# The long convolutions of a hybrid layer, emitted in two lanes of blocks that take turns

## The chip, the core and the metric

The kernel runs on one core of a Trainium2 chip. Five engines have queues of their own and execute them strictly in order: PE (matrix multiplication, writes to PSUM), DVE (vector), ACT (scalar functions), POOL (here it mostly issues DMAs) and SP (issues DMAs only). They wait for each other through semaphores. PSUM has eight banks of 128 partitions x 512 fp32 values. The metric is the device time of one execution in microseconds; less is better.

## The reference

One layer of a diffusion backbone, in fp32, on 1024 latent tokens and 256 context tokens of width 1024. One input projection makes q, k, v for 8 attention heads and three signals x1, x2, v of 512 channels for a Hyena group. The two groups of heads are independent until their outputs are concatenated:

```python
proj = h @ w_in
a = attend(q, k, v)                       # neighbourhood attention + context keys
z   = x1 * long_conv(v, k_f[:, 0])        # the Hyena group, after a width-3 convolution
hyo = x2 * long_conv(z, k_f[:, 1])
merged = concat([rmsnorm(a), rmsnorm(hyo)])
x = x + g1 * (merged @ w_out)             # then a gated FFN and the final norm
```

`long_conv` is a convolution as long as the sequence, by way of a Fourier transform: transform, multiply with the filter's spectrum, transform back. Channels don't mix in it, so it splits into blocks of 128 channels.

## The kernel before, in words

The stages, in the order in which they are written: modulated norm of the tokens; input projection, with the filters' spectra beside it; long convolutions; attention; output projection; FFN. The functions don't run as written: each engine's queue is put in order by a scheduler that works through a model of the machine and takes, of the instructions that it holds ready, the one with the highest priority, which is the order of writing. `tc.high_priority(offset=CHP)` with CHP = 2000 moves what is inside it 2000 instructions forward in that order. So the long convolutions run partly beside the projections before them and partly beside the attention after them. Once the queues are set, they don't change: an instruction that waits holds up all that stands behind it on its engine.

**One block of the long convolution** is a call of `chain(j)`: j = 0 to 3 are the four blocks of 128 channels of the latent tokens, j = 4 is all channels of the context tokens (shorter, since it needs no radix-4 steps). A block does two convolutions after each other (o = 0, then o = 1, which takes the result of the first). Each of these ten *half chains* has four phases:

- forward: 8 matmul rows on PE into the PSUM tag `cA` (`pscA`, line 802), four banks' worth, each emptied by ACT (L805, L810, L814, L815) and DVE (L816) before the next can use the bank
- spectrum: radix-4 butterflies on DVE (L822 to L827), then the product with the filter's spectrum K, which comes from DRAM in two halves through one buffer per block parity (L836; L840 to L843 on DVE)
- inverse butterflies and twiddles (L847 to L852, L857 to L859)
- inverse: 8 matmul rows (line 871) into two banks' worth of `cA`, emptied through ACT and DVE with the gate x1 or x2 (L876 to L884); for o = 1 the result goes to DRAM as `hyd` (L889, L892).

The SBUF buffers (s8, s4, t, K) carry the block's parity j % 2 in their names, so two blocks in succession have buffers of their own.

**PSUM.** While the projections run, five banks belong to them (`psp` three, `pstB` two) and three to `cA`. Attention takes seven (`psav` one, `psS` four, `psX` two), so `cA` shrinks to one. The shrinking is written in the loop over the blocks: ahead of j = 2.

**Attention** (`attend`, four calls for two heads each): scores on PE (L1038), bias and maximum on DVE (L1059, L1066), exponentials on ACT (L1072, L1073), transposes on PE (L1082) whose results ACT and DVE copy (L991, L989), products with v on PE (L999). POOL issues the loads of the bias tables (L951), of q and of k. After the four calls `token_scales` (L1187 to L1196) makes the norms of the attention's output.

**Output projection** (`psd`, L116 to L118): 480 matmuls. Its weights `w_out` come into the SBUF space that the long convolutions held (`wo_split`, L1158 on ACT, L1159 on DVE), so their loads (L1166) wait for the last block's store.

Of the kernel before, what the change touches and what calls it, by code (L numbers as in the profile page):

```python
# [77 lines left out]
def build(tc, I, O, dbg=None, upto=99):  # L78
    nc = tc.nc
    V, A, G, T, Q = nc.vector, nc.scalar, nc.gpsimd, nc.tensor, nc.sync  # L80
    dbg = dbg or {}
    top = ExitStack()
    with top:
        _build(nc, tc, top, V, A, G, T, Q, I, O, dbg, upto)


def _build(nc, tc, top, V, A, G, T, Q, I, O, dbg, upto):
# [20 lines left out]
    def bk(tag):  # L108
        pl, n, bufs = banks[tag]
        return pl.tile([P, 512 * n], F32, tag=tag, name="ps" + tag, bufs=bufs)  # L110
# [22 lines left out]
    def tw_chain(h, r):  # L133
        b = (h * 3 + r - 1) * 3
        return tw[:, b:b + 1], tw[:, b + 1:b + 2], tw[:, b + 2:b + 3]
# [364 lines left out]
    with ies:  # L500
# [3 lines left out]
        for gi, (s, col, tl) in enumerate(groups):  # L504
            xs = []
            for i in tl:
                src, row, _ = tiles[i]
# [22 lines left out]
            n = P * len(tl)  # L530
# [238 lines left out]

    def chain(j):  # L770

        lat = j < 4
        b_ = j % 2

        def s8():
            return cp.tile([P, 2048], F32, tag=f"s8{b_}", name="s8", bufs=2)

        def s4(dt=F32):
            return cp.tile([P, 1024], dt, tag=f"s4{b_}", name="s4", bufs=S4B)

        f4 = "p (h i q c) -> p h i q c"
        v2 = "p (i x) -> p i x"
        src = lxd[j] if lat else cxd
        f1 = "p i x -> p (i x)"

        def load(which):
            t = s4()
            Q.dma_start(out=t, in_=src[which].rearrange(f1))
            return t

        u = load(0)
        for o in range(2):
            uv = u.rearrange(v2, i=2)
            Gt = s8()
            Gv = Gt.rearrange(f4, h=2, i=2, q=4)
            for h in range(2):
                hs = slice(h * P, (h + 1) * P)
                for rp in range(2):
                    pa = bk("cA")
                    xs = slice(rp * 256, (rp + 1) * 256)  # L800
                    for i in range(2):
                        T.matmul(pa[:, i * 256:(i + 1) * 256], dftf[:, i, hs], uv[:, i, xs], start=True, stop=True)
                    pv = pa.rearrange("p (i r c) -> p i r c", i=2, r=2)
                    if not lat:
                        A.copy(Gv[:, h, :, 2 * rp:2 * rp + 2], pv)  # L805
                        continue
                    for ri in range(2):
                        r = 2 * rp + ri
                        if r == 0:
                            A.copy(Gv[:, h, :, 0], pv[:, :, 0])  # L810
                            continue
                        c, s, ns = tw_chain(h, r)
                        t = cp.tile([P, 2, P], F32, tag=f"t{b_}", name="t", bufs=TB)
                        A.activation(t[:, 0], pv[:, 1, ri], AF.Copy, scale=ns)  # L814
                        A.activation(t[:, 1], pv[:, 0, ri], AF.Copy, scale=s)  # L815
                        V.scalar_tensor_tensor(Gv[:, h, :, r], pv[:, :, ri], c, t, op0=ALU.mult, op1=ALU.add)  # L816
            if lat:
                ac = s4().rearrange(f4, h=2, i=2, q=2)
                X = s8()
                Xv = X.rearrange(f4, h=2, i=2, q=4)  # L820
                Xf = X.rearrange("p (h x c) -> p h x c", h=2, x=8)
                V.tensor_add(ac, Gv[:, :, :, 0:2], Gv[:, :, :, 2:4])  # L822
                V.tensor_sub(Gv[:, :, :, 2:4], Gv[:, :, :, 0:2], Gv[:, :, :, 2:4])
                V.tensor_sub(Xf[:, :, 2:8:5], Gv[:, :, :, 2], Gv[:, :, ::-1, 3])
                V.tensor_add(Xf[:, :, 3:7:3], Gv[:, :, :, 2], Gv[:, :, ::-1, 3])
                V.tensor_add(Xv[:, :, :, 0], ac[:, :, :, 0], ac[:, :, :, 1])
                V.tensor_sub(Xv[:, :, :, 1], ac[:, :, :, 0], ac[:, :, :, 1])  # L827
                Y = Gt
            else:
                X = Gt  # L830
                Y = s8()
            Xs = X.rearrange("p (h i x) -> p h i x", h=2, i=2)
            Ys = Y.rearrange("p (h i x) -> p h i x", h=2, i=2)
            for h in range(2):
                Kt = cp.tile([P, 2, 512], F32, tag=f"K{b_}", name="K", bufs=1)
                Q.dma_start(out=Kt.rearrange(f1), in_=(Kd[o, j] if lat else Kc[o])[:, h * 1024:(h + 1) * 1024])  # L836
                kr = Kt[:, 0:1].to_broadcast([P, 2, 512])
                ki = Kt[:, 1:2].to_broadcast([P, 2, 512])
                B = s4().rearrange(v2, i=2)
                V.tensor_mul(B, Xs[:, h, ::-1], ki)  # L840
                V.tensor_mul(Ys[:, h], Xs[:, h], kr)
                V.tensor_sub(Ys[:, h, 0], Ys[:, h, 0], B[:, 0])
                V.tensor_add(Ys[:, h, 1], Ys[:, h, 1], B[:, 1])  # L843
            if lat:
                ac = s4().rearrange(f4, h=2, i=2, q=2)
                Gf = Gt.rearrange("p (h x c) -> p h x c", h=2, x=8)
                V.tensor_add(ac, Gv[:, :, :, 0:4:2], Gv[:, :, :, 1:4:2])  # L847
                V.tensor_sub(Xv[:, :, :, 0:2], Gv[:, :, :, 0:4:2], Gv[:, :, :, 1:4:2])
                V.tensor_add(Gf[:, :, 1:8:6], Xv[:, :, :, 0], Xv[:, :, ::-1, 1])
                V.tensor_sub(Gf[:, :, 3:6:2], Xv[:, :, :, 0], Xv[:, :, ::-1, 1])  # L850
                V.tensor_add(Gv[:, :, :, 0], ac[:, :, :, 0], ac[:, :, :, 1])
                V.tensor_sub(Gv[:, :, :, 2], ac[:, :, :, 0], ac[:, :, :, 1])  # L852
                for h in range(2):
                    for r in (1, 2, 3):
                        c, s, ns = tw_chain(h, r)
                        t = cp.tile([P, 2, P], F32, tag=f"t{b_}", name="t", bufs=TB)
                        A.activation(t[:, 0], Gv[:, h, 1, r], AF.Copy, scale=s)  # L857
                        A.activation(t[:, 1], Gv[:, h, 0, r], AF.Copy, scale=ns)
                        V.scalar_tensor_tensor(Gv[:, h, :, r], Gv[:, h, :, r], c, t, op0=ALU.mult, op1=ALU.add)  # L859
            if o == 0:  # L860
                x1 = load(1).rearrange(v2, i=2)
                un = s4()
            else:
                x2 = load(2).rearrange(v2, i=2)
                ot = s4().rearrange(v2, i=2)
            for rp in range(2):
                pa = bk("cA")
                xs = slice(rp * 256, (rp + 1) * 256)
                for i in range(2):
                    for h in range(2):  # L870
                        T.matmul(pa[:, i * 256:(i + 1) * 256], idft[:, i, h], Ys[:, h, i, xs], start=h == 0,  # L871
                                 stop=h == 1, skip_group_check=True)
                pv = pa.rearrange(v2, i=2)
                tt = cp.tile([P, 2, 2, 256], F32, tag=f"s4{b_}", name="tt", bufs=S4B)
                if o == 0:
                    V.tensor_mul(tt[:, 0], pv, x1[:, :, xs])  # L876
                    V.tensor_mul(tt[:, 1], pv, x1[:, ::-1, xs])
                    V.tensor_add(un.rearrange(v2, i=2)[:, :, xs], tt[:, :, 0], tt[:, :, 1])
                else:
                    yt = tt[:, 0, 0]  # L880
                    A.copy(yt, pv[:, 0])
                    V.tensor_sub(ot[:, 0, xs], yt, pv[:, 1])
                    V.tensor_add(ot[:, 1, xs], yt, pv[:, 1])
                    V.tensor_mul(ot[:, :, xs], ot[:, :, xs], x2[:, :, xs])  # L884
            if o == 0:
                u = un
            elif lat:
                for i in range(2):
                    Q.dma_start(out=hyd[i * 4:i * 4 + 4, :, j * P:(j + 1) * P].rearrange("r p c -> p r c"),  # L889
                                in_=ot[:, i].rearrange("p (r c) -> p r c", r=4))  # L890
            else:
                Q.dma_start(out=hyd[8:10].rearrange("i p x -> p i x"), in_=ot)  # L892

    for j in range(5):
        if j == 2:
            cbk.close()
            cbk = Banks("bkd", "right", "tile", cA=(1, 1))
        with tc.high_priority(offset=CHP):
            chain(j)
    for _ in ada:  # L900
        pass
    scalevec(A2, n2g, 4)
# [631 lines left out]
    for f in range(NFF):  # L1534
# [7 lines left out]
        i, cs = f // 2, slice(f % 2 * 256, f % 2 * 256 + 256)  # L1542
# [239 lines left out]
```

## Time and profile before

| what | value |
|---|---|
| median of the runs | 1923.5 us (1921.77 to 1924.47, 3 runs) |
| the profiled execution's own time | 1925.38 us |
| its span | 1923.4 us |
| PE busy | 1742.3 us (91% of the span) |
| DVE busy | 1358.3 us (71%) |
| ACT busy | 893.5 us (46%) |
| POOL busy | 371.1 us (19%) |

How to read it: the span is the time from the first to the last recorded instruction; the difference of 2 us to the execution's time lies around it. Busy times are shares of the whole span, over stages that have different limits, so the argument goes by stretches of it: the projections to about 570 us, attention to about 847 us, the output projection from 937 to 1065 us, the FFN behind it. "PEclk" is the granted clock of PE, 1.00 for full speed. In a row of the timeline the first number is the start, the second the duration in us, and brackets hold the idle time ahead of it and what ended it. A matmul row of the program shows as two matmuls in the trace.

### The profile page before, as it was taken

What the parts mean: (1) busy time and instruction counts of PE and PEld (TensorE: products, weight loads), DVE (VectorE), ACT (ScalarE), POOL (GpSimd) and SP (SyncE); (2) the same over time, 40 slices, a digit from 0 to 9 for tenths busy, and PEclk for the clock granted to TensorE, in tenths of its full rate; (3) what the DMA queues carried; (4) which work ended last, traced back from release to release, by engine and by line L of the source; (5) the groups of instructions that cost most, each with busy time, mean ns of one, the idle gap of its engine ahead of it and who ended that gap; (6) DMA issues with size and microseconds to landing.
All of it is one profiled execution on the core that took longest, in us unless ns stands there. A gap on an engine that the chain in (4) does not pass through costs nothing.

```text
span 1923.4 us, 27377 instructions
## 1 busy us (share of the span) xinstructions
PE 1742.3 (91%) x9999; PEld 1460.2 (76%) x9999; DVE 1358.3 (71%) x2158; ACT 893.5 (46%) x1852; POOL 371.1 (19%) x436
## 2 busy tenths in 40 slices
PE   5899989999993798866799699999999999999997
PEld 1688877888872455443688699999999999788786
DVE  4657637756776877864455888888877777666787
ACT  4654435434342677631445544444444444443352
POOL 2354545541236553200100000000000000000001
PEclk7999989999996999985799799999999999999999
DMA  7424444456445433102622155555322222844663
GB/s 261 137 75 129 130 123 123 133 166 198 132 156 151 107 71 99 48 23 66 208 99 98 55 160 165 165 164 173 113 72 72 72 66 67 295 173 124 200 196 128
DMA packets 207288, 249.75 MB, mean 130 GB/s; under 512 B 26915, under 2 KB 152980, under 8 KB 206898
## 3 DMA queue, kind: packets, MB, share of 16 engines
q1 hardware_dynamic: 196936, 231.86, 37.5%
q0 software_dynamic: 8512, 15.33, 3.2%
q8 instruction: 79, 1.29, 0.3%
q10 hardware_dynamic: 1705, 0.82, 0.2%
q14 instruction: 56, 0.45, 0.1%
HBM read 176.75 MB, written 71.20 MB: 129 GB/s over the span
## 4 chain that ended last, share of the span: by engine, by line
PE 35%; DVE 14%; DMA 8%; issue 4%; ACT 4%; POOL 2%; SPq 0%; DVEq 0%; POOLq 0%; ACTq 0%
PE psd L118 5%; PE psd L116 5%; PE psd L117 5%; DMA wt<-in_w_down_dram 2%; PE psa L116 2%; PE psa L117 2%; PE psa L118 2%; DMA tdr<-wt 2%; POOL tb L951 2%; PE psc L117 1%; PE psc L118 1%; PE psc L116 1%; PE pscA L871 1%; PE psb L117 1%; PE psb L118 1%
## 5 line engine op out<-in xcount | busy, mean ns | idle before, releaser
L116 PE MATMUL psp<-hh,wh 128*128 128x512 f32 (+1 forms) x552 | 202.3, 367 | 2.3 <-ACT wh L121 1.9
L118 PE MATMUL psp<-hh,wl 128*128 128x512 f32 (+1 forms) x552 | 200.0, 363 | 0.9 <-POOL wl L122 0.9
L117 PE MATMUL psp<-hl,wh 128*128 128x512 f32 (+1 forms) x552 | 199.1, 361 | 0.0
L116 PE MATMUL psa<-T,ws 128*128 128x256 f32 (+1 forms) x528 | 166.2, 315 | 3.1 <-ACT rows L1497 3.0
L117 PE MATMUL psa<-T,ws 128*128 128x256 f32 (+1 forms) x528 | 165.8, 314 | 2.8 <-DVE T L1224 2.8
L118 PE MATMUL psa<-T,ws 128*128 128x256 f32 (+1 forms) x528 | 165.2, 313 | 0.0
L1697 POOL TENSOR_TENSOR rs<-rs,mhalf 128x1 f32<-128x1 f32 x10 | 7.7, 772 | 813.9 <-DVE rs L1696 813.9
L116 PE MATMUL psd<-wd,gs 128*128 128x512 f32 x360 | 140.8, 392 | 3.1 <-ACT gs L121 3.1
L117 PE MATMUL psd<-wd,gs 128*128 128x512 f32 x360 | 141.0, 392 | 0.0
L118 PE MATMUL psd<-wd,gs 128*128 128x512 f32 x360 | 123.4, 390 | 2.5 <-DVE gs L122 2.5
L116 PEld LDWEIGHTS psp<-hh,wh 128*128 128x128 f32 x552 | 105.4, 191 | 23.3 <-issue 6.2
L118 PEld LDWEIGHTS psp<-hh,wl 128*128 128x128 f32 x552 | 105.5, 191 | 16.0 <-POOL wl L122 1.2
L116 PE MATMUL psc<-T,ws 128*128 128x384 f32 (+1 forms) x352 | 110.2, 313 | 7.3 <-ACT ws L121 7.3
L117 PEld LDWEIGHTS psp<-hl,wh 128*128 128x128 f32 x552 | 105.6, 191 | 14.2 <-issue 0.4
L117 PE MATMUL psc<-T,ws 128*128 128x384 f32 (+1 forms) x352 | 110.2, 313 | 0.0
L118 PE MATMUL psc<-T,ws 128*128 128x384 f32 (+1 forms) x352 | 110.0, 313 | 0.0
L117 PE MATMUL psb<-T,ws 128*128 128x384 f32 (+1 forms) x352 | 109.9, 312 | 0.0
L118 PE MATMUL psb<-T,ws 128*128 128x384 f32 (+1 forms) x352 | 109.9, 312 | 0.0
L116 PE MATMUL psb<-T,ws 128*128 128x384 f32 (+1 forms) x352 | 109.8, 312 | 0.0
L951 POOL DMA_DIRECT2D tb<-rpw x192 | 100.4, 531 | 35.7 <-DVE m L1059 20.3
L871 PE MATMUL pscA<-s,idft 128*128 128x256 f32 x160 | 55.1, 487 | 56.0 <-DVE s L859 45.1
L116 PEld LDWEIGHTS psa<-T,ws 128*128 128x128 f32 x528 | 101.4, 192 | 4.7 <-ACT rows L1497 4.7
(394 smaller groups left out, 4800.9 us busy)
## 6 DMA issues: line engine op xcount, KB each, us to landing
wada<-in_w_ada_dram SPq DMA_DIRECT2D x48, 512.0 KB
wr<-in_w_up_dram SPq DMA_DIRECT2D x44, 512.0 KB
gr<-gdr SPq DMA_DIRECT2D x44, 320.0 KB
wr<-in_w_in_dram SPq DMA_DIRECT2D x23, 512.0 KB
wt<-in_w_down_dram SPq DMA_DIRECT2D x44, 256.0 KB
tdr<-wt SPq DMA_DIRECT2D x44, 256.0 KB
gdr<-cv SPq DMA_DIRECT2D x22, 512.0 KB
wr<-tdr SPq DMA_DIRECT2D x20, 512.0 KB
```

What stands on the lines that cost most here:

```text
L116: T.matmul(out, ah, bh, start=start, stop=False, skip_group_check=True)
L117: T.matmul(out, ah, bl, start=False, stop=False, skip_group_check=True)
L118: T.matmul(out, al, bh, start=False, stop=stop, skip_group_check=True)
L871: T.matmul(pa[:, i * 256:(i + 1) * 256], idft[:, i, h], Ys[:, h, i, xs], start=h == 0, stop=h == 1, skip_group_check=True)
L951: G.dma_start(out=tv[:, :, a * 8:a * 8 + 64], in_=rpw[var, :, 2 * p_:2 * p_ + 2, :, d * 8:d * 8 + 64].rearrange("q h u x -> q (h u) x"))
L1697: G.tensor_tensor(rs, rs, mhalf, op=ALU.pow)
```

## The change

`chain(j)` becomes a generator with a `yield` behind each of its four phases, eight per block. Two lanes are made of the blocks: 0, 2, 4 and 1, 3. A table says which lane writes its next phase: lane 0 twice, then lanes 1 and 0 in alternation, 40 turns, then lane 0 to its end. So two blocks are now written phase by phase between each other, where before one was written after the other. `cA` shrinks from three banks to one ahead of turn 16 (counted from 0), which is the last phase of block 1; block 2 has had its first forward phase by then, all of block 0 is written. No instruction of the computation is added or removed. Eight lines are added above the attention, so line 1038 becomes 1046, 1159 becomes 1167 and so on; line 802 becomes 803 and line 871 becomes 875.

```diff
@@ def chain(j):
...
                         V.scalar_tensor_tensor(Gv[:, h, :, r], pv[:, :, ri], c, t, op0=ALU.mult, op1=ALU.add)
+            yield
             if lat:
                 ac = s4().rearrange(f4, h=2, i=2, q=2)
...
                 V.tensor_add(Ys[:, h, 1], Ys[:, h, 1], B[:, 1])
+            yield
             if lat:
                 ac = s4().rearrange(f4, h=2, i=2, q=2)
...
                         V.scalar_tensor_tensor(Gv[:, h, :, r], Gv[:, h, :, r], c, t, op0=ALU.mult, op1=ALU.add)
+            yield
             if o == 0:
...
                 Q.dma_start(out=hyd[8:10].rearrange("i p x -> p i x"), in_=ot)
-
-    for j in range(5):
-        if j == 2:
+            yield
+
+
+    lanes = [(None for j in js for _ in chain(j)) for js in ((0, 2, 4), (1, 3))]
+    turn2 = [0, 0] + [1, 0] * 20 + [0] * 8
+    for n, i in enumerate(turn2):
+        if n == 16:
             cbk.close()
             cbk = Banks("bkd", "right", "tile", cA=(1, 1))
         with tc.high_priority(offset=CHP):
-            chain(j)
+            next(lanes[i], None)
```

What this does to the queues shows at three places. The first is PE's queue at the end of attention, before the change. `pscA` is a long convolution (`s_6147` belongs to block 3, the others to block 4), `psX` and `psav` are attention, L1187 its norms:

```order
L1014 MATMUL psX<-lt,sel 128x128 x4
L999 MATMUL psav<-pt,vs 64x256 x2
L1187 MATMUL psX<-ones_71,asq 128x2
L1187 MATMUL psX<-ones_71,sq 128x2
L1187 MATMUL psX<-ones_71,asq 128x2
L1187 MATMUL psX<-ones_71,sq 128x2
L871 MATMUL pscA<-s_6147,idft 128x256 x8
L802 MATMUL pscA<-s_6264,dftf 128x256 x8
L871 MATMUL pscA<-s_6283,idft 128x256 x8
L802 MATMUL pscA<-s_6300,dftf 128x256 x8
L871 MATMUL pscA<-s_6336,idft 128x256 x8
L1187 MATMUL psX<-ones_71,asq 128x2
```

And PE's queue of the change at the last rows of the same block 4, its last inverse phase (now line 875):

```order
L875 MATMUL pscA<-s_6336,idft 128x256 x2
L1007 MATMUL psav<-pt,vs 64x256 x2
L1090 MATMUL psX<-ident,Pl_6392 128x128 x2
L1090 MATMUL psX<-ident,Pl_6396 128x128 x2
L1007 MATMUL psav<-pt,vs 64x256 x2
L1090 MATMUL psX<-ident,pc 128x128 x4
L875 MATMUL pscA<-s_6336,idft 128x256 x4
L1007 MATMUL psav<-pt,vs 64x256 x2
L1090 MATMUL psX<-ident,pc 128x128 x4
```

Before, 40 rows of long convolution stand behind the last product of attention. Now the last of them has attention behind it: 88 of the 192 rows of `psav`, 194 of the 436 rows of transposes and reciprocals in `psX`, and 36 of the 144 score rows come after it.

The second place is PE's queue behind the last projection row (`psp`), before the change; `s_5566` and `s_5679` are block 1, `s_5660` its second forward phase, `s_5800` block 2:

```order
L118 MATMUL psp<-hh,wl 128x256
L871 MATMUL pscA<-s_5566,idft 128x256
L225 MATMUL pstB<-wada_7_5270,silc 32x256 x4
...
L871 MATMUL pscA<-s_5566,idft 128x256 x3
L802 MATMUL pscA<-s_5660,dftf 128x256 x2
L732 MATMUL pstB<-ident,ck 128x128 x2
L802 MATMUL pscA<-s_5660,dftf 128x256 x6
L871 MATMUL pscA<-s_5679,idft 128x256 x8
L802 MATMUL pscA<-s_5800,dftf 128x256 x2
L1038 MATMUL psS<-k,q 128x264 x2
```

And of the change; `s_5623` is the last inverse phase of block 1, `s_5863` the first forward phase of block 3:

```order
L118 MATMUL psp<-hh,wl 128x256
L225 MATMUL pstB<-wada_7_5270,silc 32x256 x4
L233 MATMUL pstB<-ident,mr_4674 128x128 x2
L671 MATMUL pstB<-ident,fo 128x128 x8
L875 MATMUL pscA<-s_5623,idft 128x256 x4
L677 MATMUL pstB<-ident,fo 128x128 x2
L875 MATMUL pscA<-s_5623,idft 128x256 x4
L732 MATMUL pstB<-ident,ck 128x128 x2
L803 MATMUL pscA<-s_5863,dftf 128x256 x4
L1046 MATMUL psS<-k,q 128x264 x2
```

Ahead of the last projection row stand 64 rows of long convolution now, and 40 before. On SP, a reload of K (L838, before L836) stands ahead of the last store of `kd` (L735) now, and behind it before. On DVE, 8 more instructions of 1024 values per partition, 18 of 512 and 20 of 256 stand ahead of the last projection's sink (L646).

The third place is DVE's queue behind the last row of block 4 (L888, before L884). L997 copies transposes for attention, L1161 copies a modulation vector into the space of `w_out`, L1167 (before L1159) splits `w_out`:

```order
L888 TENSOR_TENSOR s_6353<-s_6353,s_6351 128x2x256
L997 COPY pt<-psX 128x512
L1161 COPY sh_8282<-mods 128x16
L1015 RECIPROCAL lrow_6499<-lc 128x2 x2
L997 COPY pt<-psX 128x512
L1136 TENSOR_TENSOR at_6387<-psav,bs 128x2x16x16
L1167 SCALAR_TENSOR_TENSOR wl_8287<-wor,vec,wh_8286 128x1024
L997 COPY pt<-psX 128x512
L1167 SCALAR_TENSOR_TENSOR wl_8293<-wor,vec,wh_8292 128x1024
```

Before, all nine splits of `w_out` stood behind the end of attention and of block 4; now they stand in the last part of attention.

## The prediction

> **What bounds the kernel now.** I read the stretches first: the busy time of each engine, in order from the projections to the output projection (PE, PEld, DVE, ACT and POOL with their instruction counts, then granted clock, DMA share, GB/s).
>
> ```profile
> 440.00:500.00 60.00, 60.00 (x337) 49.18 (x337) 40.64 (x69) 27.98 (x64) 10.00 (x6) 1.00 0.44 138
> 500.00:576.00 76.00, 73.07 (x410) 58.44 (x410) 61.46 (x90) 27.82 (x66) 24.68 (x32) 1.00 0.51 162
> 576.00:600.00 24.00, 8.32 (x31) 5.94 (x29) 15.55 (x25) 7.59 (x29) 16.40 (x29) 0.76 0.64 187
> 600.00:622.00 22.00, 6.40 (x16) 3.90 (x16) 13.98 (x23) 5.02 (x14) 13.86 (x27) 0.56 0.43 113
> 622.00:847.00 225.00, 198.19 (x1263) 116.68 (x1264) 170.00 (x387) 146.41 (x474) 82.22 (x154) 0.99 0.28 72
> 780.00:820.00 40.00, 35.26 (x217) 20.20 (x215) 34.07 (x76) 29.28 (x96) 0.00 (x0) 0.96 0.13 41
> 847.00:923.00 76.00, 38.37 (x87) 23.10 (x86) 37.76 (x54) 11.49 (x25) 0.00 (x0) 0.57 0.20 62
> 923.00:937.00 14.00, 8.67 (x37) 8.52 (x37) 5.06 (x10) 5.11 (x6) 2.38 (x2) 0.50 0.56 174
> 937.00:980.00 43.00, 41.25 (x180) 33.07 (x181) 22.96 (x41) 23.97 (x41) 4.26 (x7) 0.96 0.57 200
> 1020.00:1065.00 45.00, 44.91 (x219) 36.45 (x218) 24.24 (x40) 21.66 (x38) 2.71 (x5) 1.00 0.25 88
> ```
>
> PE fills the projections (133 of 136 us), attention to 88% (198 of 225) and the output projection, 937 to 1065, nearly whole. Between them lie two holes: 576 to 622, where PE works 15 of 46 us, and 847 to 937, where it works 47 of 90, at a granted clock of 0.50 to 0.57. The timeline of PE names what stands in them:
>
> ```profile
> 570.04 0.28 PE L118 MATMUL psp<-hh,wl 128*128 128x256 f32 x1
> 613.30 1.19 PE L871 MATMUL pscA<-s,idft 128*128 128x256 f32 x2 [24.70 <-DVE s L859]
> 623.42 1.20 PE L1038 MATMUL psS<-k,q 64*128 64x264 f32 x8
> 846.08 0.65 PE L999 MATMUL psav<-pt,vs 128*64 128x256 f32 x4
> 860.23 1.22 PE L871 MATMUL pscA<-s,idft 128*128 128x256 f32 x2 [12.51 <-DVE s L859]
> 914.47 3.75 PE L871 MATMUL pscA<-s,idft 128*128 128x256 f32 x8 [1.34 <-DVE s L883]
> 936.94 0.80 PE L116 MATMUL psd<-wh,ar 128*128 128x512 f32 x1 [0.77 <-ACT ar L1251]
> ```
>
> Both holes are one block of long convolution alone: block 1 ahead of the first score, blocks 3 and 4 behind attention's last product. One block by itself is a string of dependent steps on DVE, ACT and PE, and fills none of them (DVE 38 of 76 us). The chain of waits goes on from there to the weights of the output projection:
>
> ```profile
> 914.47 3.76 PE pscA L871 x8
> 920.21 2.78 DMA hyd<-s
> 923.18 3.49 DMA wor<-in_w_out_dram
> ```
>
> So everything behind 937 waits for block 4's store and then for `w_out`, not for attention.
>
> **The change, term by term.** No work is added; what counts is where the first `psd` comes, 936.94 before. From there on PE has the same rows, so that a shift is passed on whole. I add up to that point.
>
> *Term 1, end of the projections.* Ahead of the last projection row stand 64 rows of long convolution on PE where 40 stood. What such a row costs I take from the groups of tile `pscA` alone in attention's stretch, 112 matmuls, so 56 rows, in 29.35 us of PE:
>
> ```profile
> 622.00:847.00 225.00, 29.35 (x112) 19.39 (x112) 18.43 (x37) 18.09 (x58) 0.99 0.28 72
> ```
>
> That is 0.52 us a row; 24 rows make 12.5 us, on an engine that is full there. DVE gets 8 x 1.14, 18 x 0.60 and 20 x 0.40 us more, 28 us, by these rows, of which a next instruction begins 0.08 us before the end:
>
> ```profile
> 573.04 0.48 DVE L646 SCALAR_TENSOR_TENSOR cv<-psp,vec,cv 128x255 f32<-128x255 f32 x1
> 604.15 1.23 DVE L840 TENSOR_TENSOR s<-s,K 128x1024 f32<-128x1024 f32 x1 [3.35 <-DMA K<-Kd]
> 605.29 1.22 DVE L841 TENSOR_TENSOR s<-s,K 128x1024 f32<-128x1024 f32 x1
> 606.54 0.69 DVE L842 TENSOR_TENSOR s<-s,s 128x512 f32<-128x512 f32 x1
> ```
>
> With the 100 us that it has from 440 to 573 that is 128 us in 146, or 88%, fuller than in either row above (68% and 81%); the sinks of the projections stand in that queue, and PE waits for their banks. Bounds: 12.5 us, if PE alone decides, and 25 us, if DVE gets no fuller than 81% (128 / 0.81 = 158). I take 19.5, between the two, since both engines are near their end: the last sink ends at 573 + 20 = 593.
>
> *Term 2, from there to the first score.* On DVE stand 8 instructions of 1024, 14 of 512 and 13 of 256 (22.7 us) and one reload of K, 3.35 us by the row above. SP's order has that reload ahead of the last store of `kd`, which attention's k waits for; both end together. With some 2 us of handovers 28 us: first score on DVE at 621, where PE had its first at 623 before. The first hole shrinks, and the longer projections take what it gives. From below 23 us (DVE alone), from above the 48 us that block 1 took there before.
>
> *Term 3, attention beside the convolutions.* From the first score to block 4's last row DVE has 32 chain instructions of 1024, 68 of 512 and 46 of 256 values: 36.5 + 40.8 + 18.4 = 96 us. Of attention it has 48 of the 64 biases and 12 of 16 maxima, 18 of 32 copies, and small ones. By these groups (busy us, mean ns)
>
> ```profile
> L1059 DVE CUSTOM_DVE_ANT_0 Pl<-psS,tb 128x264 f32<-128x264 f32 (+3 forms) x64 | 28.9, 486 | 2.7 <-PE psS L1038 2.3 <-DMA q<-qd 0.3
> L989 DVE COPY pt<-psX 128x512 f32<-128x512 f32 x32 | 21.9, 683 | 5.6 <-PE psX L1082 5.6
> L1066 DVE TENSOR_REDUCE n<-psS 128x4 f32<-128x1024 f32 x16 | 19.5, 1217 | 1.1 <-PE psS L1038 1.1
> ```
>
> less the 0.08 us each they are 24.5 + 13.7 + 10.8 us, the small ones 11: 60 us. Sum 156 us. PE has 84 chain rows (44 us) and attention's part: 198 - 29 = 169 us in all, less 67 for what comes later (next term), so 146 us. DVE is the fuller one. How full can it get? Before 76% on the average (170 of 225), 85% from 780 to 820 (34.07 of 40), and once, for 20 us, without a gap:
>
> ```profile
> 780.00:800.00 20.00, 17.56 (x116) 9.76 (x114) 20.00 (x40) 10.35 (x32) 0.00 (x0) 1.00 0.25 80
> ```
>
> Two blocks that don't wait for each other give it more to choose from; I take 90%, between the second and the third: 173 us. Bounds: 95% (164 us) and the old 76% (205 us). Block 4 ends at 621 + 173 = 794.
>
> *Term 4, the rest of attention alone.* 46% of `psav`, 44% of `psX`, 25% of the scores remain: 67 of 169 us of PE. At 95% 71 us; at the 88% of before 76. In its first part DVE and ACT now stand behind `w_out`: the copy at L1161 waits for block 4's store (2.78 us in the chain of waits), the first split for the first load (3.49 us), and the loads go through two buffers. That cover is PE's stock of finished transposes, two banks; I count 8 us, between nothing and the 14 us of the stretch 923 to 937, which was that wait laid open. End of attention: 794 + 71 + 8 = 873.
>
> *Term 5, norms of attention to the first `psd`.* Of 923 to 937, 14 us, the norms are the main part; the weights lie ready now, so 13 us: 886.
>
> **Sum:** 936.9 - 886 = 51 us gained; of the profiled execution's 1925.4 us 1874.4 remain. That execution lay 1.9 us over the median of 1923.5, so 1872.5 is the number to compare: 1872 us.
>
> **The clock.** Term 3 rests on PE's clock staying at 0.99, as in the row 622 to 847, with a single `cA` bank cycling there too. The Trainium skill, page "TensorE: Matmul & The Clock Gate", section "A second HAM failure mode: psum-queue depth-cycling", tells of a kernel whose clock swings between half and full speed, since PE idles briefly between bursts into PSUM banks. By that page the interleaved stretch would run at a lower clock; the trace so far disagrees with it for this kernel (0.99). It is the last rival below.
>
> **Rivals.**
>
> *The bank round trip decides.* In term 3, 18 forward and 12 inverse passes go one after another through the one `cA` bank. What a pass takes beside attention:
>
> ```profile
> 685.96 1.03 PE L802 MATMUL pscA<-s,dftf 128*128 128x256 f32 x4
> 690.30 1.13 PE L802 MATMUL pscA<-s,dftf 128*128 128x256 f32 x4
> 756.41 1.13 PE L802 MATMUL pscA<-s,dftf 128*128 128x256 f32 x4
> 763.68 1.03 PE L802 MATMUL pscA<-s,dftf 128*128 128x256 f32 x4
> ```
>
> From 4.3 to 7.3 us. At 4.3 the 30 passes are 129 us, and hidden; at 7.3 they are 219 us in place of 173: 1918 us. For it speaks that two blocks on one fuller DVE lengthen each emptying; against it that the passes of one block fall into the DVE phases of the other. 9%.
>
> *The projections pay.* Weight loads stand behind K loads on SP, and the sinks behind block 0's and 1's products on DVE. Then the last sink is 30 us late and not 20, and the first score, too: 1882 us. The chance is 12%.
>
> *More is gained.* DVE at 97% in term 3 (161 us), nothing lost in term 4 and 12.5 us in term 1: 12 + 8 + 7 = 27 us more, 1845 us. For it speaks the row from 780 to 800, against it that DVE kept this up for 20 us only. 8%.
>
> *Slower: PE's clock falls while the two lanes alternate.* The mechanism is there in the holes: 0.56 from 600 to 622, 0.57 from 847 to 923, where PE was a third to a half busy. In term 3 PE would be 146 of 173 us busy, 84%, less than the 88% of before. At half clock its 146 us become 292: block 4 ends at 913, the rest follows as above, 79 + 13 us, and the time is 1992 us. It decides from where PE's work outlasts the 173 + 51 us that are to be had, a mean clock below 146 / 224 = 0.65. Against it: from 780 to 820 the clock was 0.96 with PE at 88%. 3%.
>
> *The change does nothing at the end:* block 4 would have to come last again. The queue's order excludes it, and I give it no chance of its own.
>
> **How the numbers follow.** Forecast (the long convolutions end under attention, 20 to 77 us gained): 68%, and the rivals 9, 12, 8 and 3%. The bounds of terms 1, 3 and 4 give 7 + 9 + 8 = 24 us below; those of 1 to 4 give 5.5 + 20 + 32 + 11 = 68 us above, hardly all at once; with half of the bank rival left out above and part of the gain rival below, the range is 1846 to 1904 us. A measurement of this kernel tells 0.2%, 3.8 us, from no change: faster means below 1919.7. Forecast, projections, gain and half of the bank rival are faster: 0.93; the other half is mostly the same, 0.03; clock and the bank's far end slower, 0.04.
>
> **What would show it.** First `psd` near 886; the stretch of DVE alone without PE behind attention gone, and `w_out` split before attention ends. Term 1: the last `psp` near 583 to 595. Term 3: DVE at 85% or more between the first score and block 4's store, PE's clock at 0.95 or more. Term 4: a wait of DVE's copy for `hyd`, then PE near 95%. It would be wrong if `cA`'s matmuls wait on PE for their bank, some 2 us each in 30 passes, or if the granted clock in attention falls under 0.9.

## The result and the profile after

The change makes the kernel faster: 1872.7 us median (1869.7 to 1876.3) where the kernel before took 1922.6 us (1915.5 to 1924.5) beside it, a ratio of 0.9748 with a 95% interval of 0.9715 to 0.9780. The profiled execution took 1869.67 us, its span 1867.9 us; before 1925.38 and 1923.4 us.

The stretches after, in the same columns as in the prediction (window, busy time of PE, PEld, DVE, ACT and POOL with counts, clock, DMA share, GB/s):

```profile
500.00:585.00 85.00, 78.09 (x435) 63.35 (x433) 73.03 (x114) 38.93 (x105) 27.05 (x34) 0.99 0.44 141
585.00:615.00 30.00, 14.82 (x42) 9.35 (x40) 24.18 (x41) 9.71 (x35) 13.30 (x22) 0.64 0.75 231
615.00:797.00 182.00, 152.36 (x854) 93.97 (x854) 154.54 (x329) 106.24 (x345) 94.97 (x179) 0.91 0.39 102
797.00:874.00 77.00, 66.22 (x457) 38.13 (x453) 38.84 (x86) 48.76 (x131) 3.86 (x8) 1.00 0.21 66
874.00:887.00 13.00, 9.56 (x44) 9.36 (x44) 1.46 (x7) 2.77 (x4) 2.38 (x2) 0.59 0.11 37
887.00:930.00 43.00, 43.00 (x192) 34.82 (x193) 17.62 (x36) 20.51 (x37) 4.34 (x8) 0.96 0.45 154
```

The hole of 847 to 937, in which PE worked 47 of 90 us, is gone. What is left between attention and the output projection are the 13 us of the norms. The hole ahead of attention is 30 us long (585 to 615) where it was 51 (573 to 624). The timeline of PE at the joints:

```profile
578.87 0.28 PE L118 MATMUL psp<-hh,wl 128*128 128x256 f32 x1
602.57 2.05 PE L803 MATMUL pscA<-s,dftf 128*128 128x256 f32 x4 [8.76 <-DMA s<-lxd]
609.44 2.21 PE L1046 MATMUL psS<-k,q 64*128 64x264 f32 x8
793.68 1.89 PE L875 MATMUL pscA<-s,idft 128*128 128x256 f32 x8
886.77 0.77 PE L116 MATMUL psd<-wh,ar 128*128 128x512 f32 x1
```

and of DVE, where the last sink of the projections, the first bias of attention, block 4's last row and the first step of the `w_out` split stand:

```profile
584.93 0.48 DVE L646 SCALAR_TENSOR_TENSOR cv<-psp,vec,cv 128x255 f32<-128x255 f32 x1
615.21 0.43 DVE L1067 CUSTOM_DVE_ANT_0 Pl<-psS,tb 128x264 f32<-128x264 f32 x1
796.85 0.69 DVE L888 TENSOR_TENSOR s<-s,s 128x512 f32<-128x512 f32 x1
800.60 0.26 DVE L1161 COPY sh<-mods 128x16 f32<-128x16 f32 x1 [0.79 <-DMA hyd<-s]
```

The first output projection row moved from 936.94 to 886.77, by 50.2 us, and the median by 50.0. Block 4 ends 75 us ahead of attention (872 us), so its store and the weights no longer stand between attention and the output projection.

### The profile page after: what moved, and what is told of

Same layout as the page of the kernel before. It is cut to its first block, busy times and chain, and to the rows that moved or that the text cites. A ratio compares the mean times of both kernels' runs of the same rounds, so it can differ in the third digit from the quotient of the medians.

```text
span 1867.9 us, 27370 instructions
## 1 busy us (share of the span) xinstructions
PE 1731.8 (93%) x9999; PEld 1459.0 (78%) x9999; DVE 1359.7 (73%) x2158; ACT 892.7 (48%) x1852; POOL 373.9 (20%) x436
## 4 chain that ended last, share of the span: by engine, by line
PE 50%; DVE 14%; DMA 6%; ACT 5%; issue 3%; POOL 1%; SPq 0%; DVEq 0%; POOLq 0%; ACTq 0%
PE psd L118 6%; PE psd L116 6%; PE psd L117 6%; PE psa L116 3%; PE psa L117 2%; PE psa L118 2%; DMA wt<-in_w_down_dram 2%; PE psc L117 2%; PE psc L118 2%; PE psc L116 2%; PE psav L1007 2%; PE psb L117 2%; PE psb L118 2%; PE psb L116 2%; DMA tdr<-wt 2%
## 5 line engine op out<-in xcount | busy, mean ns | idle before, releaser
L116 PEld LDWEIGHTS psp<-hh,wh 128*128 128x128 f32 x552 | 105.4, 191 | 24.5 <-issue 6.6
L116 PE MATMUL psc<-T,ws 128*128 128x256 f32 (+1 forms) x352 | 110.0, 313 | 8.0 <-ACT ws L121 8.0
L117 PE MATMUL psc<-T,ws 128*128 128x256 f32 (+1 forms) x352 | 110.0, 313 | 0.0
L118 PE MATMUL psc<-T,ws 128*128 128x384 f32 (+1 forms) x352 | 109.5, 312 | 0.0
L116 PEld LDWEIGHTS psa<-T,ws 128*128 128x128 f32 x528 | 101.2, 192 | 3.4 <-ACT rows L1505 3.2
L117 PEld LDWEIGHTS psa<-T,ws 128*128 128x128 f32 x528 | 101.2, 192 | 3.1 <-DVE T L1232 3.1
```

Source lines behind the costliest of these rows:

```text
L116: T.matmul(out, ah, bh, start=start, stop=False, skip_group_check=True)
L117: T.matmul(out, ah, bl, start=False, stop=False, skip_group_check=True)
L118: T.matmul(out, al, bh, start=False, stop=stop, skip_group_check=True)
```

## Experiments

Every run stood beside the kernel before on its chip; ratios are to that kernel's runs. The table gives the medians and, from each profile, the starts of five rows: the last sink of the projections and the first bias of attention on DVE, and on PE the last row of the long convolutions, the last product of attention (`psav`) and the first row of the output projection.

| kernel | median us | ratio (95% interval) | last sink | first bias | last `pscA` | last `psav` | first `psd` |
|---|---|---|---|---|---|---|---|
| before | 1922.6 | 1 | 573.0 | 624.3 | 914.5 | 846.1 | 936.9 |
| the change | 1872.7 | 0.9748 (0.9715–0.9780) | 584.9 | 615.2 | 793.7 | 872.2 | 886.8 |
| 1 bank point alone | 1931.9 | 1.0065 (1.0040–1.0089) | 568.6 | 595.7 | 920.5 | 856.1 | 943.1 |
| 2 lanes alone | 1876.1 | 0.9766 (0.9742–0.9789) | 588.1 | 617.3 | 794.0 | 874.1 | 888.5 |
| 3 lanes early | 1901.6 | 0.9898 (0.9875–0.9921) | 584.9 | 608.0 | 892.6 | 872.5 | 915.1 |
| 4 lanes late | 1866.3 | 0.9717 (0.9694–0.9741) | 571.7 | 623.1 | 856.4 | 861.7 | 879.9 |
| 5 load on ACT | 1872.4 | 0.9768 (0.9745–0.9792) | 585.8 | 616.1 | 793.5 | 872.9 | 887.3 |
| 6 more on DVE | 1882.8 | 0.9820 (0.9798–0.9843) | 589.7 | 619.5 | 810.1 | 883.1 | 897.5 |
| 7 more on PE | 1877.8 | 0.9795 (0.9772–0.9819) | 590.7 | 619.2 | 804.4 | 881.5 | 895.9 |
| 8 half a block apart | 1892.1 | 0.9863 (0.9843–0.9883) | 590.5 | 625.6 | 854.9 | 890.4 | 906.1 |
| 9 change, tables in order | 1873.5 | 0.9753 (0.9735–0.9772) | 589.5 | 619.8 | 810.6 | 872.3 | 886.7 |
| 10 as 1, tables in order | 1930.7 | 1.0059 (1.0038–1.0080) | 572.0 | 601.1 | 919.2 | 856.6 | 941.6 |
| 11 as 8, tables in order | 1886.8 | 0.9818 (0.9796–0.9839) | 589.5 | 624.5 | 855.3 | 882.4 | 898.6 |
| 12 as 3, tables in order | 1901.5 | 0.9894 (0.9873–0.9915) | 587.3 | 610.1 | 889.1 | 866.1 | 911.2 |

In all variants the scheduler orders the queues anew, so none moves one thing alone. The profiles also scatter: PE's queue up to the last projection row is the same in the change and in runs 6 and 9, and has one row of long convolution more in run 2, and the last sink came at 584.9, 589.7, 589.5 and 588.1; from the first `psd` to the end of the span the profiles took between 981.1 (the change) and 986.5 us (before), with the same rows there. Stretches between two rows of one profile are therefore compared below, and times by their ratios.

### The two parts apart: runs 1 and 2

The bank point is the turn at which `cA` shrinks to one bank. Run 1 writes the blocks one after another and has the bank point of the change; run 2 keeps the lanes and shrinks `cA` when blocks 0 and 1 are written whole.

```diff
# run 1
-    lanes = [... for js in ((0, 2, 4), (1, 3))]
-    turn2 = [0, 0] + [1, 0] * 20 + [0] * 8
+    lanes = [... for js in ((0, 1, 2, 3, 4),)]
+    turn2 = [0] * 40
     for n, i in enumerate(turn2):
-        if n == 16:
+        if n == 15:
# run 2
-        if n == 16:
+        if n == 17:
```

Expected of run 1:

> Blocks written one after another as before; only the point where cA shrinks from three banks to one is that of the change, ahead of the last phase of block 1. Theory (the gain comes from two blocks filling each other's waits, so that nothing of block 3 and 4 is left alone behind attention): 40 rows of long convolution still stand behind the last product of attention, the first row of the output projection comes at 937 as before, 1922 us, at most 6 us to either side. Rival (the gain is the two banks that attention gets earlier): 1890 us or less.

Expected of run 2:

> Two lanes as in the change, but cA shrinks when blocks 0 and 1 are written whole (one turn later), as the kernel before has it. Theory: 1873 us, within 6 us, since only one inverse phase gets its banks in another way. Rival (the bank point carries the gain): 1890 us or more.

The lanes alone make the gain, 0.9766. The bank point alone does not make any; it costs 0.65%, some 12 us, which neither side had expected; within the lanes it makes no difference that shows (0.9748 and 0.9766). PE in run 1, from the first score on:

```profile
583.32 1.38 PE L1046 MATMUL psS<-k,q 64*128 64x264 f32 x8
596.61 2.08 PE L1046 MATMUL psS<-k,q 64*128 64x256 f32 x8 [11.91 <-DVE m L1067]
606.28 1.55 PE L1046 MATMUL psS<-k,q 64*128 64x352 f32 x4 [7.59 <-DVE m L1067]
856.07 0.65 PE L1007 MATMUL psav<-pt,vs 128*64 128x256 f32 x4
943.06 0.80 PE L116 MATMUL psd<-wh,ar 128*128 128x512 f32 x1 [0.78 <-ACT ar L1259]
```

The banks come free 40 us earlier and the first score with them (583 for 623), but the second waits 11.91 us and the third 7.59 us for DVE, whose queue has products of the long convolutions ahead of the biases. The product rows of attention end 10 us later than before, with 10 rows of long convolution more (64 for 54) between first score and last product: 5 us at 0.52 us a row. An early first score ended nothing early.

### Where the overlap pays: runs 3 and 4

```diff
# run 3: blocks 0 and 1 take turns, then 2, 3, 4 in series
+    lanes = [... for js in ((0, 2, 3, 4), (1,))]
+    turn2 = [0, 0] + [1, 0] * 6 + [1, 1] + [0] * 24
+        if n == 15:
# run 4: blocks 0, 1 in series, 2 and 3 take turns, then 4
+    lanes = [... for js in ((0, 1, 2, 4), (3,))]
+    turn2 = [0] * 18 + [1, 0] * 8 + [0] * 10
+        if n == 16:
```

Expected of run 3:

> Only blocks 0 and 1 take turns (beside the projections), blocks 2, 3 and 4 follow one after another. 57 rows of long convolution stand ahead of the last projection row (40 before, 64 with the change), and 16 behind the last product of attention, the second half chain of block 4. Theory: attention has 24 rows more beside it, 14 us (24 x 0.52 / 0.88), and ends at 861; behind it one half chain alone, 23.4 us by the rows 896.79 to 920.21 of the kernel before, then store and weights, 16.7 us as before: first row of the output projection at 900, 1880 to 1892 us, so two thirds of the gain, all from what was moved out of the hole at the end. Rival (the gain is that the first hole, ahead of the first score, closes, or that the overlap of blocks 2 to 4 alone counts): 1915 us or more.

Expected of run 4:

> Blocks 0 and 1 one after another as before, only blocks 2 and 3 take turns, block 4 follows. 40 rows of long convolution stand ahead of the last projection row as before, none behind the last products of attention. Theory: the projections end at 573 as before, attention with 40 rows more beside it (40 x 0.52 / 0.88 = 24 us) ends at 871, block 4 with it, so that the wait for its store and the weights is only partly covered, and the norms: first row of the output projection at 887 to 895, 1873 to 1881 us. Rival (it is the work moved ahead of the last projection row that pays): 1905 us or more.

Run 3 gained 1.0%, 20 us, of the forecast 31 to 43. Behind attention's last product it took 42.6 us to the first `psd`, where 39 were expected; the rest of the miss is attention itself, which ended at 872 and not at 861 although its first bias came 16 us earlier than before. As in run 1 the early start was worth nothing. Run 3 has run 1's bank point, ahead of block 1's last phase, and run 4 that of the kernel before, so the 12 us that the bank point cost in run 1 may be part of run 3's miss; early turns with the old bank point were not tried.

Run 4 is the fastest kernel here: 1866.3 us (1863.1 to 1871.9), faster than the 1873 to 1881 us expected of it, since attention ended at 862 and not at 871. On the same chip run 2, the lanes of the change, took 1876.1 us (1871.6 to 1879.4), and the two intervals of the ratio just don't touch (0.9694 to 0.9741, 0.9742 to 0.9789). Against the change's own interval, from another set of runs, it isn't apart. Attention in run 4:

```profile
623.00:660.00 37.00, 30.23 (x179) 17.16 (x176) 30.08 (x73) 23.40 (x81) 20.83 (x40) 1.00 0.37 94
623.00:862.00 239.00, 212.53 (x1332) 129.66 (x1328) 201.63 (x437) 154.75 (x496) 82.06 (x154) 0.99 0.32 85
```

and with the change, its first 37 us and the whole:

```profile
615.00:652.00 37.00, 24.60 (x100) 14.80 (x100) 31.36 (x57) 15.81 (x52) 25.01 (x48) 0.72 0.37 86
615.00:873.00 258.00, 217.58 (x1297) 131.10 (x1298) 193.38 (x414) 154.99 (x474) 98.82 (x186) 0.93 0.34 91
```

From first bias to last product run 4 needs 239 us with 94 rows of long convolution behind its first score, the change 257 us with 84. Between these two windows PE's idle time fell from 40 to 26 us and its busy time by 5, at a clock of 0.99 for 0.93. In run 4 DVE is 84% busy over the whole of it. With the change it is 85% busy to 797 and 50% from there on (38.84 of 77), since the convolutions, most of whose work is on DVE, come first and leave attention alone. Run 4 pays for this at the end, where block 4's store and the weights lie open again:

```profile
860.77 4.61 DMA hyd<-s
...
873.85 4.30 DMA wor<-in_w_out_dram
```

(from its chain of waits; the first `psd` follows at 879.88, 23.5 us after the last `pscA` row.) So the turns of blocks 0 and 1 beside the projections, half of the change, are not needed for the gain: turns of 2 and 3 bring all of it without them.

### The wait for block 3's load: run 5

```diff
-            Q.dma_start(out=t, in_=src[which].rearrange(f1))
+            (A if which == 0 and j > 1 else Q).dma_start(out=t, in_=src[which].rearrange(f1))
```

> The change, with the first load of a block (u, for blocks 2, 3 and 4) issued by ACT in place of SP, so that block 3's load no longer stands behind the reload of K and the store of kd; the queues of PE, DVE and POOL are those of the change. Theory (the wait of 8.76 us on PE for block 3's load makes the first hole longer): that wait is gone, the first score on PE comes 3 to 6 us earlier than 609.4, and the time is 2 to 6 us less than the change's 1872.7. Rival (the hole is set by DVE's products and the reload of K, 5.85 us, and the wait for the load lies beside them): first score and time within 2 us.

The time stayed, as the rival had it, but this does not show the rival's reason, since the wait is still there.

```profile
603.49 2.05 PE L803 MATMUL pscA<-s,dftf 128*128 128x256 f32 x4 [8.88 <-DMA s<-lxd]
610.38 2.21 PE L1046 MATMUL psS<-k,q 64*128 64x264 f32 x8
```

ACT issues the load at the moment at which DVE has finished the addition of line 887, block 1's (rows of ACT's queue, then of DVE):

```profile
597.78 0.33 ACTq L789 DMA_DIRECT2D s<-lxd  x1
```

```profile
597.29 0.41 DVE L887 TENSOR_TENSOR s<-tt,pscA 128x256 f32<-128x256 f32 x1
```

and with the change it was the same: that row ran from 596.48 to 596.89, and SP issued the load at 596.92. Block 3's load waits for an SBUF buffer that block 1 still holds (three buffers, `S4B`, for each parity of the blocks), and not for its queue. What this hole would be worth isn't measured by this run, and a fourth buffer was not tried.

### Which engine sets the stretch: runs 6 and 7

```diff
# run 6 (the second product overwrites the first)
+                if j >= 2:
+                    V.tensor_mul(Ys[:, h], Xs[:, h], ki)
                 V.tensor_mul(Ys[:, h], Xs[:, h], kr)
# run 7
                         T.matmul(pa[:, i * 256:(i + 1) * 256], dftf[:, i, hs], ...)
+                        if j >= 2 and h == 0:
+                            T.matmul(pa[:, i * 256:(i + 1) * 256], dftf[:, i, hs], ...)
```

Expected of run 6:

> The change, with one product of 1024 values on DVE done twice in each half of the spectrum of blocks 2, 3 and 4: 12 x 1.14 = 13.7 us more on DVE, nothing more on PE. Theory of the prediction (DVE sets the length of the stretch in which attention and convolutions alternate): block 4 ends 13 to 16 us later, and the time is 10 to 16 us more. Rival (PE, over that stretch and the rest of attention together, sets the end): PE does more of attention in the longer stretch and has less left, 0 to 5 us more.

Expected of run 7:

> The change, with half of the forward matmul rows of blocks 2, 3 and 4 done twice into the same bank: 24 rows more, 12.5 us at 0.52 us a row or 14.4 us at 0.60, nothing more on DVE. Theory of the prediction (DVE sets the stretch, PE has 30 us of it idle): 0 to 6 us more. Rival (PE over the whole of attention sets the end): 12 to 17 us more, 14.4 us and what its 85% makes of it.

On the same chip run 5, which takes the change's time, had 1872.4 us. DVE's 13.7 us cost 10.4 us, and the intervals of the ratio are apart; PE's 12.5 to 14.4 us cost 5.4 us, with intervals that overlap. The stretch from first bias to block 4's last row (the first row of each fence) and the rest of attention:

```profile
619.00:815.00 196.00, 164.53 (x912) 99.62 (x913) 169.07 (x347) 113.60 (x365) 99.06 (x186) 0.90 0.35 96
815.00:884.00 69.00, 61.06 (x392) 33.56 (x392) 36.36 (x81) 44.37 (x116) 0.00 (x0) 0.95 0.21 69
```

is run 6, and run 7:

```profile
619.00:808.00 189.00, 162.97 (x899) 102.36 (x899) 155.22 (x331) 110.61 (x360) 96.00 (x181) 0.90 0.35 98
808.00:882.00 74.00, 64.96 (x436) 36.06 (x434) 38.72 (x87) 46.49 (x121) 3.06 (x6) 1.00 0.20 68
```

Against the change's 182.3 us the first stretch is 12.2 us longer with more on DVE, which stays 86% busy, and 7.4 us longer with more on PE. So DVE sets it for the most part, and PE is no bystander, though only 20 of the 24 doubled rows stand behind the first score. The doubled rows also hold the one `cA` bank longer, but PE's waits for that bank did not grow by them (10.4 us in all in this stretch, 13.4 with the change). But from first bias to first `psd` only 6.5 and 5.2 us of that remain: where the first stretch gets longer, PE does more of attention in it (116 product rows ahead of the last `pscA` row in run 6, 104 with the change) and has less left. The two terms of the prediction were not independent. The rest of run 6's 10.7 us at the first `psd` is its later first bias, which is within the scatter told above.

### Half a block apart, and the order of the bias tables: runs 8 to 12

Run 8 writes lane 0 four phases ahead (`turn2 = [0] * 4 + [1, 0] * 20`, `cA` shrunk at turn 18).

> Two lanes whose blocks stand half a block apart (lane 0 is written four phases ahead and not two), so that block 4's first half alternates with block 3's second half; cA shrinks two turns later, at turn 18. The queue on PE has 64 rows ahead of the last projection row as with the change, 65 ahead of the first score (76 with the change), and 44 of 192 product rows of attention behind the last row of block 4 (88 with the change). Theory: the sum of the work between the projections and the output projection is the same, and the wait for the weights (38 us from block 4's store to the last split with the change) still lies under the rest of attention: 1865 to 1880 us. Rival (what decides is how much of attention is left to cover the weights): 1885 us or more.

It lost 20 us of the gain, and its time lies in the rival's range. Yet from attention's last product to the first `psd` it takes 15.7 us, with the change 14.6, so the weights lengthened what stands behind attention by 1 us only. They are close behind it, though: the chain of waits that ends at the first `psd` runs through their loads, from the first to the last,

```profile
864.58 4.36 DMA wor<-in_w_out_dram
...
890.99 3.34 DMA wor<-in_w_out_dram
```

while attention's last product starts at 890.4. Whether the splits of `w_out`, which stand among attention's last copies, held attention up is not shown. Besides, run 8 has a later first bias (35 us behind the last sink and not 30) and a longer attention (264.7 us from first bias to last product, not 257.0).

POOL's queue offered a cause. With the change, and in runs 1 to 3 and 5 to 8, four loads of the second head pair's bias table stand ahead of the first pair's 32 remaining ones, and wait until DVE has used the table once; before, and in run 4, they don't. POOL with the change:

```profile
616.30 18.76 POOL L959 DMA_DIRECT2D tb<-rpw  x36 [10.47 <-DVE m L1067]
```

Runs 9 to 12 hold the second pair's loads behind the first pair's, in the change and in the variants of runs 1, 8 and 3:

```diff
-            for var in range(3):
-                bias_load(p_, var)
+            with tc.issue_after(tlast[0].ins) if p_ == 1 else ExitStack():   # tlast: the latest table load
+                for var in range(3):
+                    bias_load(p_, var)
```

> The change, with the loads of the second head pair's bias tables held, on POOL's queue, behind the last table load of the first pair; with the change four of them stand ahead of the first pair's 32 remaining loads and wait for DVE's first use of the table. Theory (this order throttles the first 40 us of attention, 24.6 of 37 us of PE busy at a clock of 0.72 where the kernel before has 29.4 of 37 at 1.00): the 32 loads are issued from 606 on and not from 618, PE gets back 5 to 10 us in that stretch, 1860 to 1868 us. Rival (DVE, 85% busy there, has the same work to do in any order): 1870 us or more.

> Blocks one after another and cA shrunk at the change's point, as in the run of the bank point alone (1932 us), with the table loads in order. Theory: the 10 us that the bank point cost there came from the order of the table loads: 1915 to 1925 us. Rival (the single bank ahead of block 1's last phase costs it by itself): 1929 us or more.

> Lanes half a block apart (1892 us) with the table loads in order; 40 of 192 product rows of attention are left behind block 4's last row. Theory (the table loads cost what this variant lost): 1872 to 1882 us. Rival (too little attention is left to cover the weights of the output projection): 1885 us or more.

> Only blocks 0 and 1 taking turns (1901.6 us) with the table loads in order; block 4's second half chain and the end of its first still stand behind attention. Theory: 6 to 12 us less, 1889 to 1896 us. Rival (the shortfall there came from elsewhere): 1899 us or more.

In run 9 only 5 of the 32 loads start earlier; the other 27 start at 619.44, where with the change the 32 follow four loads from 616.30 on:

```profile
610.38 2.11 POOL L961 DMA_DIRECT2D tb<-rpw  x4
615.37 0.53 POOL L961 DMA_DIRECT2D tb<-rpw  x1 [2.88 <-DMA k<-kd]
619.44 20.29 POOL L961 DMA_DIRECT2D tb<-rpw  x39 [3.54 <-DMA vs<-vd]
```

and the stretch that they were to speed up is what it was, PE 24.19 us of 37 where it was 24.60 (24.74 when counted from run 9's own later first bias, 620 to 657):

```profile
615.00:652.00 37.00, 24.19 (x103) 14.44 (x100) 31.07 (x57) 15.75 (x51) 22.91 (x44) 0.73 0.46 114
```

The change, run 1 and run 3 take the same time with the tables in order, so the order that was written is not what costs them. That the tables' time of arrival costs nothing is not shown by this, since most of the loads came no earlier in run 9, nor in run 12. DVE was 84 to 85% busy in that stretch in both, as the rival had it, and 81% in run 4 (30.08 of 37). What differs from run 4 is the work that was done: from 570 to 660 the change ran 88 matmuls of `pscA` and 90 of attention on PE, run 4 78 and 155. Only in run 8's variant did the order cost something that shows, 0.9863 to 0.9818, and there half of the 32 loads (16) did come ahead of the first bias. From first bias to last product all four got shorter, by 4.5, 4.8, 6.8 and 8.5 us (runs 9 to 12 against the change and runs 1, 8 and 3), but three of the four did not end measurably earlier; where that goes is not shown beyond the scatter. Of the 13 us that run 11 still takes more than run 9, 5 lie ahead of its first bias, 5 in its attention and 2 behind it; the cause stays open.

## Why the prediction came out right

The time, 1872 us, was met, and its mechanism holds: blocks 3 and 4 alone behind attention were the loss, run 2 shows that the lanes bring the gain, and run 4 that the late blocks' overlap is enough for all of it. But that the sum came out to 1 us is luck: two terms were wrong in size, term 1 by 8 us too much and term 3 by 9 us too little, and cancelled.

**Term 1** was mis-sized, the last sink at 593. The profile has 584.9, 11.9 us late and not 20, below even the lower bound of 12.5. Of the 48 matmuls more (24 rows) 12 had found room ahead of 440. The other 36 cost PE 8.7 us (tile `pscA`, before and then the change):

```profile
440.00:570.00 130.00, 20.18 (x80) 14.50 (x80) 12.64 (x26) 13.51 (x44) 1.00 0.49 156
```

```profile
440.00:579.00 139.00, 28.85 (x116) 21.03 (x116) 18.62 (x37) 18.46 (x60) 1.00 0.47 153
```

That is by how much the last projection row came later (578.87 for 570.04). DVE was 86% busy from 500 to 585 (73.03 of 85 us), fuller than the 81% of the upper bound. The scatter matters here: over the three profiles with this queue (the change and runs 6 and 9) the last sink is at 588.0 on the mean, over the four with the old one (before and runs 1, 4 and 10) at 571.3. That is 16.7 us, nearer to the forecast than the one profile says.

**Term 2**, 28 us from there to the first bias, was 30.3. Most of it is DVE (24.2 us busy) and K's reload (3.2 us) as said; its upper bound of 48 us is 50 by the rows shown for block 1 (573.04 to 623.42). Block 3's load waits for a buffer of block 1, which the term did not have.

**Term 3** had DVE's sum nearly right (156 us forecast, 154.5 measured), in part by luck: its 24.5 us for 48 biases do not come out of the row, which gives 48 x 0.41 = 19.5 and a sum of 151. It had the share wrong, 85% for 90%: 182 us for 173. With the first bias 6 us earlier than forecast (615 for 621) and 9 us more here, block 4 ended at 797 and not at 794. No run shows DVE above 86% over the whole of such a stretch; the row of 20 us without a gap was no measure for 180 us.

**Term 4**, 79 us for the rest of attention, was 76; DVE's wait for `hyd` was 0.79 us and ACT's waits for `w_out` 3.7 us in all, so the 8 us counted for them were too much, while PE kept to 86% (66.2 of 77), near the 88% of before, and did not reach 95%. **Term 5** fits: 13 us. The shift was passed on as said; that the profile took 5.3 us less behind the first `psd` (981.1 for 986.5) lies within the scatter of the profiles.

**The rivals.** The bank round trip did not decide: PE waited for a `cA` bank 13.4 us in all between first bias and block 4's last row,

```profile
PE pscA L803 <- DVE s L817: 8.4, 3, 5.8
PE pscA L875 <- DVE s L817: 2.5, 1, 2.5
PE pscA L803 <- DVE tt L881: 1.9, 1, 1.9
PE pscA L875 <- DVE tt L881: 0.6, 1, 0.6
```

(us in total, times, longest), and not 2 us in each of 30 passes. What the forecast missed is the clock, said to be 0.95 or more. It was 0.91 in the stretch, just above the 0.9 named as a sign of being wrong, and a matmul of `pscA` took 0.30 us and not 0.26:

```profile
615.00:797.00 182.00, 49.60 (x164) 32.83 (x164) 19.47 (x39) 17.19 (x48) 0.91 0.39 102
```

That is 7 us of PE; how much of it reached the time is not measured. Over the stretch the rival's 0.65 was not near; most of the loss is in the first 37 us (0.72), where PE was busy for 24.6.

The Trainium skill, page "TensorE: Matmul & The Clock Gate", section "A second HAM failure mode: psum-queue depth-cycling", puts such a clock down to short pauses of PE between bursts into banks that take turns. The trace agrees in part: the clock was low where PE paused for DVE (0.54 from 640 to 650, with one pause of 5.75 us), but in run 4 one bank cycles just the same, and the clock is 0.99.

## What to carry to other kernels

A string of dependent steps that stands alone behind a full stage costs its whole length; written in turns with a second such string, so that both end under the stage, it costs little. The turns pay where the strings would have stood alone (here the late blocks, 2.8% in run 4); turns of the early blocks beside a stage that already fills PE brought 1.0% by themselves (run 3), and nothing that shows on top of the late ones (the change against run 4). A consumer's first row that comes earlier in a fixed queue is no gain by itself: look whether its second row then waits, and compare where the stage ends.

## What was not expected of the hardware

PE's granted clock was lower where PE paused more, here in two stretches of 37 us: 1.00 with PE 30.2 of 37 us busy (run 4, 623 to 660), 0.72 with 24.6 of 37 (the change, 615 to 652), with one `cA` bank in both, though a different mix of rows. And kernels with the same PE queue up to a row in the middle of the program differ by up to 5 us at its sink (584.9 with the change, 589.7 in run 6), so that a stage's shift of that size, read from one profile each, is not yet an effect.
